# Second block: where the convolution's taps and its layer norm run, and a third buffer for loaded weights

## The chip, the cores and the metric

The kernel runs on 1 core of one Trainium2 chip. The metric is the device time of one execution in microseconds (us), a median of runs. The engines are TensorE (PE in the rows; its weight loads PEld), VectorE (DVE), ScalarE (ACT), GpSimd (POOL) and SyncE (SP), which issues nearly all DMAs in one queue, in order.

## What is computed

Three transformer-like blocks stand one behind the other, on 1024 positions of width 1024 in float32. The change touches the second block:

```python
def second_block(x, norm_g, w_in, ...):
    h = rmsnorm(x, norm_g[l])
    z = h @ w_in[l]
    qa, ka, va, glu_a, glu_b, pool_in, sgu_u, sgu_v, gates = jnp.split(z, split_at, axis=-1)
    y_a = neighborhood_attention(qa, ka, va, na_rpb[l])
    y_b = conformer_conv(glu_a, glu_b, ...)
    y_c = multiscale_pool(pool_in, pool_w[l], pool_scale[l])
    y_d = spatial_gating(jax.nn.gelu(sgu_u), jax.nn.gelu(sgu_v), ...)
    y = jnp.concatenate([y_a, y_b, y_c, y_d], axis=-1) * jax.nn.silu(gates)
    x = x + y @ w_out[l]
    return rmsnorm(x, final_g)

def conformer_conv(a, b, dw_w, dw_b, ln_g, ln_b, pw):      # 256 channels, CONV_WIDTH = 31
    h = a * jax.nn.sigmoid(b)
    h = lax.conv_general_dilated(h, dw_w[:, None, :], ..., feature_group_count=h.shape[-1]) + dw_b
    h = jax.nn.silu(layernorm(h, ln_g, ln_b))
    return h @ pw
```

## The kernel before

Activations lie feature-major: 128 features on the partitions, 1024 positions along the free axis, handled in two halves `h` of 512. Every float32 product is made of three TensorE matmuls, of a high and a low part of weights and activations (`mm3`, L190 to L192). `dense` makes one output tile of 128 x 512 from eight such triples, 24 matmuls; `dense_tm` the same for a tile with positions on the partitions, 128 x 256.

**Weights.** In the second block the weights have been split into high and low parts earlier and lie in DRAM (`wsplit`). `ready` (L159) loads one weight, 512 KB high and 512 KB low, into tiles with the tags `whi` and `wlo` of the pool `wp`, which has two buffers for each tag. A weight therefore waits until the last but one has been used. The first and third blocks use `chunk` (L147) instead: it loads an unsplit weight under the tag `raw` (two buffers of the same size), and ScalarE and VectorE or GpSimd split it into `whi` and `wlo`. Over the second block the two `raw` buffers hold the third block's first two weights.

**The second block's stages**, in program order: for each half the GLU (`glu`: two dense tiles for each of two channel groups `b`, hp = pa * sigmoid(pb)), the values of the attention (`values`, stored to `vd`), the queries and keys (`qk`, stored to `qkd`); then the pooling branch (`px`, `s2`, `s4`, `pls`), the gating's layer norm (`v2`: eight tiles of 128 x 256, `dense_tm`, Gelu into one of two `sq` buffers, then `layer_norm` on VectorE with one power on GpSimd), the loads of the attention's operands from `qkd` (`stacks(0)`, L1114, 32 DMAs of 32 x 1024), the convolution's layer norm and its 256 x 256 product (L1245 to L1272), two gate blocks (L1274 to L1289, weights 10 and 11, four dense tiles in all), and `silu(f)`, eight gates of two dense tiles each, which multiply what the branches stored in `yd`. The neighbourhood attention follows: 2 head groups x 2 bands x 4 column tiles x 4 heads, 64 score tiles of 128 x 384. A score tile is a product (L1368), bias and maximum on VectorE (L1371), an exponential on ScalarE, reciprocal and scaling on VectorE, three transposes (L1379), a copy on ScalarE, and a share of the product with the values (L1386). The bias tiles are loaded in a ring of four and get their mask on GpSimd (L1361). The table `more` puts `silu` 7, 2, 3, 0 and 1 in between the score tiles; 4, 5 and 6 stand ahead of them. Sixteen dense tiles of the output projection (`out`, with `mix`) end the block.

**The taps.** The convolution is a generator, `taps`: one tap of the centre on ScalarE (L1126), and 30 for each of two channel groups. Of these 60, 40 are one VectorE instruction each, `ca += hp * w` (L1138). The 20 with `j % 3 == 0` are a ScalarE product into a `tap` tile, which has one buffer (L1135), and a GpSimd addition into `cb` (L1136); `cb` is added to `ca` at the end (L1141). `fill(n)` takes n taps out of the generator wherever it is called.

**What sets the order.** The source order gives each instruction its place only roughly: the program is built under a scheduler that puts each engine's instructions into one fixed sequence, with priorities by program order. On the chip each engine then runs its own sequence in order, and a waiting instruction holds everything behind it on its engine. The same goes for SP's queue of DMA issues.

## Time and profile before

| | us |
|---|---|
| median of 3 runs | 3373.1 (3364.29 to 3378.03) |
| the profiled execution | 3371.98 |
| its span, first to last instruction | 3370.2 |
| TensorE busy in it | 3177.4 (94%) |
| VectorE, ScalarE, GpSimd busy | 2073.7, 1480.9, 633.5 |
| mean granted TensorE clock | 0.973 |

Times inside the profile are us from the span's start. Granted clock 1.00 is 2.4 GHz, 0.50 is 1.2 GHz, the lower level. The second block runs from about 1250 to 1800; its pooling, convolution and gate stages lie between 1345 and 1567, its attention between 1567 and 1737. A matmul's record is longer than the step to the next one, since matmuls are pipelined, so that a busy TensorE is not one at its peak.

### The profile page before, as it was taken

How to read it: one execution, taken by the hardware profiler on the slowest of the kernel's cores; microseconds unless marked ns; L12 is line 12 of the kernel's file. 1: busy time of each engine (PE TensorE's matmuls, PEld its weight loads, DVE VectorE, ACT ScalarE, POOL GpSimd, SP SyncE). 2: the span in 40 equal slices, each digit the busy share in tenths (PEclk: the TensorE clock that was granted, in tenths of full speed). 3: DMA queues.
4: the chain of work that ended last, by engine and by line, in shares of the span. 5: the costliest groups of instructions: out<-in, count | busy, mean ns of one | idle time of the engine just before them, and what ended most of it. 6: DMA issues, size and time to landing. Idle time of an engine off the chain costs nothing.

```text
span 3370.2 us, 43537 instructions
## 1 busy us (share of the span) xinstructions
PE 3177.4 (94%) x16068; PEld 2647.5 (79%) x16068; DVE 2073.7 (62%) x3779; ACT 1480.9 (44%) x2678; POOL 633.5 (19%) x427
## 2 busy tenths in 40 slices
PE   7999999999999998879999899989899999999997
PEld 6789877788888887667677778778887778888886
DVE  8666666554446554953666575675735587887436
ACT  5454553455543222322544465554534444545312
POOL 3000024000000001521213454445323200000001
PEclk9999999999999999889999899999999999999999
DMA  4112124433489726546765221224513333222433
GB/s 131 42 54 63 57 100 160 133 107 120 131 318 352 275 80 217 175 142 216 208 237 165 63 69 60 82 91 144 169 57 119 122 112 105 79 91 94 133 113 105
DMA packets 173989, 445.73 MB, mean 132 GB/s; under 512 B 22736, under 2 KB 31312, under 8 KB 169680
## 3 DMA queue, kind: packets, MB, share of 16 engines
q1 hardware_dynamic: 173776, 442.96, 40.4%
q8 instruction: 126, 2.06, 0.3%
q14 instruction: 87, 0.71, 0.1%
HBM read 329.63 MB, written 106.43 MB: 129 GB/s over the span
## 4 chain that ended last, share of the span: by engine, by line
PE 72%; DVE 12%; DMA 7%; ACT 4%; issue 3%; POOL 1%; SPq 0%; DVEq 0%; ACTq 0%; POOLq 0%
PE ps_d L190 21%; PE ps_d L192 21%; PE ps_d L191 21%; DVE ca L1138 2%; DMA wlo<-wsplit 1%; ACT whi L143 1%; DMA nq<-upd 1%; DVE wlo L145 1%; DVE act L145 1%; POOL wlo L145 1%; PE ps_o L1386 1%; DMA wsplit<-w 1%; DVE acc L1520 1%; PE ps_t L1379 1%; DMA w<-in_w_fm 1%
## 5 line engine op out<-in xcount | busy, mean ns | idle before, releaser
L190 PE MATMUL ps_d<-act,whi 128*128 128x512 f32 x1344 | 540.0, 402 | 40.1 <-DMA whi<-wsplit 24.0
L192 PE MATMUL ps_d<-act,wlo 128*128 128x512 f32 x1344 | 535.2, 400 | 7.6 <-DVE wlo L145 4.0
L191 PE MATMUL ps_d<-act,whi 128*128 128x512 f32 x1344 | 536.2, 399 | 0.1
L143 ACT ACTIVATE whi<-raw 128x1024 fp32r<-128x1024 f32 (+2 forms) x282 | 268.5, 953 | 537.9 <-PE ps_d L191 442.6
L192 PE MATMUL ps_d<-up,wlo 128*128 128x512 f32 x864 | 336.7, 390 | 2.7 <-DVE wlo L145 2.7
L145 POOL TENSOR_TENSOR wlo<-raw,whi 128x1024 fp32r<-128x1024 f32 (+1 forms) x110 | 265.9, 2420 | 384.1 <-ACT whi L143 366.9
L190 PE MATMUL ps_d<-up,whi 128*128 128x512 f32 x864 | 336.4, 390 | 0.1
L191 PE MATMUL ps_d<-up,whi 128*128 128x512 f32 x864 | 336.4, 390 | 0.0
L190 PEld LDWEIGHTS ps_d<-act,whi 128*128 128x128 f32 x1344 | 258.7, 192 | 98.7 <-issue 33.4
L191 PE MATMUL ps_d<-act,ws 128*128 128x512 f32 x812 | 316.3, 389 | 0.0
L192 PE MATMUL ps_d<-act,ws 128*128 128x512 f32 x812 | 314.4, 390 | 0.0
L190 PE MATMUL ps_d<-act,ws 128*128 128x512 f32 x812 | 312.7, 390 | 0.4 <-ACT ps_d L856 0.4
L192 PEld LDWEIGHTS ps_d<-act,wlo 128*128 128x128 f32 x1344 | 257.7, 192 | 65.1 <-DMA wlo<-wsplit 6.7
L191 PEld LDWEIGHTS ps_d<-act,whi 128*128 128x128 f32 x1344 | 258.4, 192 | 53.2 <-issue 1.1
L230 POOL TENSOR_TENSOR rr<-rv,mhalf 128x4 f32<-128x4 f32 (+1 forms) x43 | 45.6, 1059 | 1165.0 <-DVE rv L220 978.9
L145 DVE TENSOR_TENSOR wlo<-raw,whi 128x1024 fp32r<-128x1024 f32 (+2 forms) x172 | 176.5, 1026 | 108.5 <-ACT whi L143 108.1
L192 PE MATMUL ps_d<-mix,wlo 128*128 128x512 f32 x512 | 203.5, 398 | 5.6 <-POOL wlo L145 4.7
L190 PE MATMUL ps_d<-mix,whi 128*128 128x512 f32 x512 | 201.9, 400 | 5.6 <-DVE acc L646 4.3
L191 PE MATMUL ps_d<-mix,whi 128*128 128x512 f32 x512 | 204.4, 399 | 0.7 <-DVE mix L145 0.6
L192 PEld LDWEIGHTS ps_d<-up,wlo 128*128 128x128 f32 x864 | 162.3, 188 | 38.0 <-DVE wlo L145 4.2
L190 PEld LDWEIGHTS ps_d<-up,whi 128*128 128x128 f32 x864 | 162.3, 188 | 33.7 <-ACT whi L143 0.6
L191 PEld LDWEIGHTS ps_d<-up,whi 128*128 128x128 f32 x864 | 162.3, 188 | 33.4
(440 smaller groups left out, 6619.2 us busy)
## 6 DMA issues: line engine op xcount, KB each, us to landing
raw<-in_w_up SPq DMA_DIRECT2D x90, 512.0 KB, 3.9
wsplit<-w SPq DMA_DIRECT2D x32, 1024.0 KB, 5.8
raw<-in_w_fm SPq DMA_DIRECT2D x56, 512.0 KB, 3.9
upd<-c SPq DMA_DIRECT2D x108, 256.0 KB, 3.0
nq<-upd SPq DMA_DIRECT2D x108, 256.0 KB, 3.6
whi<-wsplit SPq DMA_DIRECT2D x50, 512.0 KB, 4.5
wlo<-wsplit SPq DMA_DIRECT2D x50, 512.0 KB, 5.5
xd<-acc SPq DMA_DIRECT2D x80, 256.0 KB, 3.2
```

The lines of the kernel that those rows point to most:

```text
L143: nc.scalar.activation(hi, src, AF.Copy)
L145: e.tensor_tensor(lo, src, hi.bitcast(F32), op=ALU.subtract)
L190: nc.tensor.matmul(out, lhsT=wh, rhs=xh, start=start, stop=False, skip_group_check=more)
L191: nc.tensor.matmul(out, lhsT=wh, rhs=xl, start=False, stop=False, skip_group_check=more)
L192: nc.tensor.matmul(out, lhsT=wl, rhs=xh, start=False, stop=stop, skip_group_check=more)
L230: self.nc.gpsimd.tensor_tensor(r, v, self.mhalf.broadcast_to([P, n]), op=ALU.pow)
L1138: nc.vector.scalar_tensor_tensor(ca[b][:, dst], hx[b][:, src], w, ca[b][:, dst], op0=ALU.mult, op1=ALU.add)
L1379: nc.tensor.transpose(tp[:, blk(kb)], pr[:, blk(kb)], e.ident)
L1386: nc.tensor.matmul(po[32 * hd : 32 * hd + 32, :P], lhsT=va[ct][:, band + kb, blk(hd, 32)], rhs=pts[hd][:, blk(kb)], start=kb == 0, stop=kb ...
L1520: nc.vector.scalar_tensor_tensor(m, m, g[:, k : k + 1], r, op0=ALU.mult, op1=ALU.mult)
```

## The change

Three things are edited. `ready` now turns among three places: two are the `whi`/`wlo` pairs, the third is the pair of `raw` buffers. All 60 taps are VectorE instructions, and the `fill` calls are given other counts and two more places (gate blocks, first `silu`). The convolution's layer norm and product become a generator `conv_rest`, of which two steps at a time are taken behind the halves of `silu` 5, 6 and 7; `silu(7)` moves ahead of the attention, and `silu` 2 and 3 trade places in `more`.

```diff
     def ready(self, src, shape=(8, P)):
 
-        self.turn = (self.turn + 1) % (2 + len(self.wx))
-        wp = self.wp if self.turn < 2 else self.wx[0]
+        self.turn = (self.turn + 1) % 3
         out = []
         for i, t in enumerate(("whi", "wlo")):
-            w = wp.tile([P] + list(shape), F32R, tag=t, name=t)
+            w = self.wp.tile([P] + list(shape), F32R, tag=t if self.turn < 2 else "raw", name=t)
...
         def taps():
+            w = lambda b, i: cv[:, b * 34 + i : b * 34 + i + 1]
             for b in range(2):
-                w = lambda i: cv[:, b * 34 + i : b * 34 + i + 1]
-                nc.scalar.activation(ca[b], hx[b], AF.Identity, bias=w(31), scale=w(15))
-                nc.gpsimd.memset(cb[b], 0.0)
+                nc.scalar.activation(ca[b], hx[b], AF.Identity, bias=w(b, 31), scale=w(b, 15))
             for j in range(15):
                 for b in range(2):
                     for d in (j - 15, 15 - j):
...
-                        if j % 3 == 0:
-                            t = odd.tile([P, T], F32, tag="tap", name="tap")[:, src]
-                            nc.scalar.activation(t, hx[b][:, src], AF.Copy, scale=w)
-                            nc.gpsimd.tensor_tensor(cb[b][:, dst], cb[b][:, dst], t, op=ALU.add)
-                        else:
-                            nc.vector.scalar_tensor_tensor(ca[b][:, dst], hx[b][:, src], w, ca[b][:, dst], op0=ALU.mult, op1=ALU.add)
+                        nc.vector.scalar_tensor_tensor(ca[b][:, dst], hx[b][:, src], w(b, d + 15), ca[b][:, dst], op0=ALU.mult, op1=ALU.add)
                         yield
-            for b in range(2):
-                nc.vector.tensor_tensor(ca[b], ca[b], cb[b], op=ALU.add)
...
                 qk(1, i, h)
-                fill(1)
+                fill(3)
...
                 nc.scalar.activation(x[:, half(h)], e.dense(w, hs[h]), AF.Copy)
-                fill(1)
+                fill(2)
...
-        fill(99)
         st = stacks(0)
-
-
-        cw = e.kept(io["conv_pw_2"], 2, 256)
-        for h in range(2):
...
                 nc.sync.dma_start(yd[6 + b, :, h], t)
+                fill(4)
+
+
+        def conv_rest():
+            cw = e.kept(io["conv_pw_2"], 2, 256)
+            for h in range(2):
+                bk = [e.pt() for _ in range(2)]
+                xn = e.slot("xn", (4, 256))
+                for t in range(4):
...
+                    layer_norm(e, tp[:, :256], xn[:, t], LN)
+                    for b in range(2):
+                        nc.tensor.transpose(bk[b][:, blk(t)], xn[:, t, blk(b)], e.ident)
+                    yield
...
-        for f in (4, 5, 6):
-            silu(f)
+        silu(4, lambda: fill(5))
+        fill(99)
+        steps = conv_rest()
+
+        def hook():
+            for _ in range(2):
+                next(steps, None)
+
+        for f in (5, 6, 7):
+            silu(f, hook)
+        for _ in steps:
+            pass
...
-        more = {(0, 0): (7,), (0, 1): (2, 3), (1, 0): (0, 1)}
+        more = {(0, 0): (2,), (0, 1): (3,), (1, 0): (0, 1)}
```

Three places show what becomes of this in the engines' sequences. The first is SP's queue around `stacks(0)`: `st` are the attention's operands, `lw` the gating's parameters, `yd` a branch's stored result. Before:

```order
L173 DMA nt<-in_conv_pw 128x512
L1220 DMA yd_10678<-nt 128x512
L1114 DMA st_12212<-qkd_10679 32x1024 x4
L1114 DMA st_12213<-qkd_10679 32x1024 x4
L1114 DMA st_12214<-qkd_10679 32x1024 x4
L1114 DMA st_12215<-qkd_10679 32x1024 x4
L1114 DMA st_12232<-qkd_10679 32x1024 x4
L1114 DMA st_12233<-qkd_10679 32x1024 x4
L1114 DMA st_12234<-qkd_10679 32x1024 x4
L1114 DMA st_12235<-qkd_10679 32x1024 x4
L166 DMA whi<-wsplit 128x1024
L166 DMA wlo<-wsplit 128x1024
```

SP's queue at the same place, changed:

```order
L165 DMA whi<-wsplit 128x1024
L165 DMA wlo<-wsplit 128x1024
L1209 DMA yd_10678<-nt 128x512 x3
L1215 DMA lw<-in_sgu_ln 128x512
L1216 DMA lw<-in_sgu_w 128x512
L1113 DMA st_12137<-qkd_10679 32x1024
L1209 DMA yd_10678<-nt 128x512
L1113 DMA st_12137<-qkd_10679 32x1024 x3
L1113 DMA st_12138<-qkd_10679 32x1024 x4
```

The weight of the first gate block, which stood behind the 32 loads, now stands ahead of the pooling's stores; the second gate block's weight stays behind them.

The second place is SP's queue where the third block's first two weights are loaded (`raw<-in_w_fm`). Before, that is at the start of the second block:

```order
L1229 DMA bst<-in_sgu_b 128x256
L152 DMA raw<-in_w_down 128x640 x20
L152 DMA raw<-in_w_fm 128x1024
L1054 DMA xd_10665<-acc 128x512 x2
L152 DMA raw<-in_w_fm 128x1024
L166 DMA whi<-wsplit 128x1024
L166 DMA wlo<-wsplit 128x1024
```

In the changed program they stand at the end of the second block, behind its last weight:

```order
L165 DMA whi<-wsplit 128x1024
L165 DMA wlo<-wsplit 128x1024
L1593 DMA xd_14985<-acc 128x512
L1622 DMA lvf<-in_c_levels 128x448
L1593 DMA xd_14985<-acc 128x512
L152 DMA raw<-in_w_fm 128x1024 x4
```

That last weight is the 50th which `ready` loads, and by the turn among three places it is one of those in the `raw` pair.

The third place is TensorE's sequence at the first score tiles of the attention. Before, the tiles stand between the matmuls of a `silu` tile (`ps_d<-act`):

```order
L190 MATMUL ps_d<-act,whi 128x512
L1386 MATMUL ps_o<-probT,va 32x128 x2
L1368 MATMUL ps_s<-st_12232,st_12212 128x384
L1368 MATMUL ps_s<-st_12233,st_12213 128x384
L191 MATMUL ps_d<-act,whi 128x512
L192 MATMUL ps_d<-act,wlo 128x512
L190 MATMUL ps_d<-act,whi 128x512
L1379 MATMUL ps_t<-ident,pr 128x128 x6
```

Changed, the first six tiles stand alone:

```order
L1371 MATMUL ps_s<-st_12157,st_12137 128x384
L1371 MATMUL ps_s<-st_12158,st_12138 128x384
L1371 MATMUL ps_s<-st_12159,st_12139 128x384
L1371 MATMUL ps_s<-st_12160,st_12140 128x384
L1382 MATMUL ps_t<-ident,pr 128x128 x6
L1389 MATMUL ps_o<-probT,va 32x128
L1371 MATMUL ps_s<-st_12157,st_12137 128x384
L1371 MATMUL ps_s<-st_12158,st_12138 128x384
L1389 MATMUL ps_o<-probT,va 32x128
L1382 MATMUL ps_t<-ident,pr 128x128 x6
L1389 MATMUL ps_o<-probT,va 32x128
L189 MATMUL ps_d<-act,whi 128x512
```

Six of the ten `silu` tiles that stood among the first 24 score tiles now stand ahead of the attention; the remaining four stand among score tiles 6 to 12, and tiles 12 to 44 have none, where before that was so for tiles 24 to 44.

## Rows read from the trace of the kernel before

**Rows 1.** Busy by stretch: us, PE, PEld, DVE, ACT, POOL, clock, DMA share, GB/s

```profile
1299.00:1345.00 46.00, 38.89 (x201) 32.86 (x200) 15.14 (x22) 8.42 (x17) 6.27 (x5) 0.93 0.67 217
1345.00:1424.00 79.00, 64.72 (x292) 52.84 (x290) 76.26 (x47) 25.91 (x32) 37.91 (x15) 0.87 0.57 174
1424.00:1482.00 58.00, 49.73 (x302) 44.53 (x300) 44.28 (x100) 19.75 (x29) 21.43 (x18) 0.97 0.43 130
1482.00:1500.00 18.00, 5.53 (x18) 4.17 (x19) 5.34 (x14) 0.57 (x1) 2.19 (x5) 0.54 1.02 267
1500.00:1567.00 67.00, 65.42 (x340) 53.34 (x339) 20.06 (x38) 15.91 (x24) 5.78 (x6) 1.00 0.53 171
1567.00:1640.00 73.00, 73.00 (x410) 56.26 (x409) 37.60 (x109) 30.17 (x74) 16.94 (x9) 1.00 0.69 215
1640.00:1680.00 40.00, 31.63 (x219) 20.53 (x218) 26.70 (x86) 22.67 (x63) 13.07 (x7) 0.83 0.73 212
...
1670.00:1710.00 40.00, 38.13 (x278) 25.34 (x268) 37.46 (x110) 28.65 (x78) 14.87 (x8) 0.98 0.59 187
```

**Rows 2.** TensorE's waits, 1299 to 1345 first, then 1345 to 1540: total, times, longest

```profile
PE ps_d L190 <- DMA whi<-wsplit: 4.1, 2, 3.3
...
PE ps_d L190 <- DMA whi<-wsplit: 20.6, 4, 9.1
PE ps_t L1258 <- DVE xn L1037: 5.1, 1, 5.1
PE ps_s L190 <- ACT pls L143: 4.8, 2, 4.5
```

**Rows 3.** SP's queue in order of time: start, us until issued, what

```profile
1366.14 4.14 SPq L1082 DMA_DIRECT2D vd<-nt  x6
...
1385.87 9.50 SPq L1104 DMA_DIRECT2D qkd<-qk  x2
...
1474.37 16.64 SPq L1114 DMA_DIRECT2D st<-qkd  x32
1491.84 0.34 SPq L166 DMA_DIRECT2D whi<-wsplit  x1
```

**Rows 4.** One line's instructions: count, ns min/median/max, first and last start, forms

```profile
L1138 DVE SCALAR_TENSOR_TENSOR ca<-hp,g_conv_par,ca x40: 1259/1274/3440, 1347.5 to 1424.5; 128x1010 f32<-128x1010 f32 x4, 128x1011 f32<-128x1011 f32 x4, 128x1013 f32<-128x1013 f32 x4, 128x1014 f32<-128x1014 f32 x4
L1141 DVE TENSOR_TENSOR ca<-ca,cb x2: 1218/1222/1226, 1443.7 to 1451.7; 128x1024 f32<-128x1024 f32 x2
L1210 DVE SCALAR_TENSOR_TENSOR nt<-s,g_c_iw,px x8: 743/751/2872, 1437.4 to 1466.7; 64x512 f32<-64x512 f32 x8
```

**Rows 5.** Groups, 1250 to 1900: busy us, mean ns of one, idle before

```profile
L1138 DVE SCALAR_TENSOR_TENSOR ca<-hp,g_conv_par,ca 128x1010 f32<-128x1010 f32 (+9 forms) x40 | 73.3, 1870 | 1.7 <-ACT ca L1126 1.3
...
L1135 ACT ACTIVATE tap<-hp,g_conv_par 128x1009 f32<-128x1009 f32 (+4 forms) x20 | 22.8, 1139 | 23.7 <-POOL cb L1136 23.7
```

**Rows 6.** The chain that ended last, start and us; then GpSimd's instructions

```profile
1347.55 1.28 DVE ca L1138
...
1348.86 2.88 DVE ca L1138
...
1353.07 3.27 DVE ca L1138
...
1348.69 1.97 POOL L1136 TENSOR_TENSOR cb<-cb,tap 128x1009 f32<-128x1009 f32 x1 [32.45 <-ACT tap L1135]
1351.91 3.35 POOL L1136 TENSOR_TENSOR cb<-cb,tap 128x1009 f32<-128x1009 f32 x1 [1.25 <-ACT tap L1135]
```

**Rows 7.** TensorE's instructions one by one: start and us

```profile
1340.16 0.40 PE L191 MATMUL ps_d<-act,whi 128*128 128x512 f32 x1
...
1355.37 0.39 PE L192 MATMUL ps_d<-act,wlo 128*128 128x512 f32 x1
...
1659.42 0.69 PE L1368 MATMUL ps_s<-st,st 128*128 128x384 f32 x1 [6.61 <-DVE mx L1371]
```

**Rows 8.** Score tiles on VectorE, 1567 to 1640, then 1670 to 1710

```profile
L1371 DVE CUSTOM_DVE_ANT_0 pr<-ps_s,bias x22: 551/557/559, 1567.6 to 1636.3; 128x384 f32<-128x384 f32 x22
...
L1371 DVE CUSTOM_DVE_ANT_0 pr<-ps_s,bias x23: 530/547/558, 1671.5 to 1709.3; 128x384 f32<-128x384 f32 x23
```

**Rows 9.** DMA issues of the page: KB each, us to landing; a split on ScalarE

```profile
raw<-in_w_fm SPq DMA_DIRECT2D x56, 512.0 KB, 3.9
...
1828.53 1.05 ACT L143 ACTIVATE whi<-raw 128x1024 fp32r<-128x1024 f32 x1
```

More of the change, by code (lines that the diff above doesn't have):

```diff
@@ L153, in chunk @@
         self.turn = (self.turn + 1) % (2 + len(self.wx))
-        wp = self.wp if self.turn < 2 else self.wx[0]
+        wp = self.wx[0] if self.wx and self.turn == 2 else self.wp
         hi, lo = (wp.tile(shape, F32R, tag=t, name=t) for t in ("whi", "wlo"))
@@ L159, in ready @@
     def ready(self, src, shape=(8, P)):
-        self.turn = (self.turn + 1) % (2 + len(self.wx))
-        wp = self.wp if self.turn < 2 else self.wx[0]
+        self.turn = (self.turn + 1) % 3
         out = []
         for i, t in enumerate(("whi", "wlo")):
-            w = wp.tile([P] + list(shape), F32R, tag=t, name=t)
+            w = self.wp.tile([P] + list(shape), F32R, tag=t if self.turn < 2 else "raw", name=t)
             self.nc.sync.dma_start(w.bitcast(F32), src[:, i].rearrange("p (a b) -> p a b", a=shape[0]))
@@ L1119, in block2 @@
         ca = [e.slot("ca", (T,)) for _ in range(2)]
-        cb = [e.slot("cb", (T,)) for _ in range(2)]
         hx = [t.rearrange("p a b -> p (a b)") for t in hp]
         def taps():
+            w = lambda b, i: cv[:, b * 34 + i : b * 34 + i + 1]
             for b in range(2):
-                w = lambda i: cv[:, b * 34 + i : b * 34 + i + 1]
-                nc.scalar.activation(ca[b], hx[b], AF.Identity, bias=w(31), scale=w(15))
-                nc.gpsimd.memset(cb[b], 0.0)
+                nc.scalar.activation(ca[b], hx[b], AF.Identity, bias=w(b, 31), scale=w(b, 15))
             for j in range(15):
@@ L1243, in block2 @@
             fill(1)
-        fill(99)
         st = stacks(0)
-        cw = e.kept(io["conv_pw_2"], 2, 256)
-        for h in range(2):
-            bk = [e.pt() for _ in range(2)]
-            xn = e.slot("xn", (4, 256))
-            for t in range(4):
-                tp = e.pss()
-                for b in range(2):
-                    nc.tensor.transpose(tp[:, blk(b)], ca[b][:, blk(4 * h + t)], e.ident)
-                layer_norm(e, tp[:, :256], xn[:, t], LN)
-                for b in range(2):
-                    nc.tensor.transpose(bk[b][:, blk(t)], xn[:, t, blk(b)], e.ident)
-            hl = []
-            for b in range(2):
-                o = b * 34
-                t = e.tnt()
-                nc.scalar.activation(t, bk[b], AF.Silu, bias=cv[:, o + 33 : o + 34], scale=cv[:, o + 32 : o + 33])
-                y = e.split_slot(t, "cs")
-                hl.append((y[:, 0], y[:, 1]))
-            for f in range(2):
-                p = e.pss()
-                for b in range(2):
-                    e.mm3(p, (cw[0][:, b, blk(f)], cw[1][:, b, blk(f)]), hl[b], b == 0, b == 1)
-                t = e.tnt()
-                nc.scalar.activation(t, p, AF.Copy)
-                nc.sync.dma_start(yd[2 + f, :, h], t)
         for b in range(2):
@@ L1289, in block2, with silu @@
                 nc.sync.dma_start(yd[6 + b, :, h], t)
+                fill(4)
[5 more added lines that the diff above has]
+                for t in range(4):
+                    tp = e.pss()
+                    for b in range(2):
+                        nc.tensor.transpose(tp[:, blk(b)], ca[b][:, blk(4 * h + t)], e.ident)
+                    layer_norm(e, tp[:, :256], xn[:, t], LN)
+                    for b in range(2):
+                        nc.tensor.transpose(bk[b][:, blk(t)], xn[:, t, blk(b)], e.ident)
+                    yield
+                hl = []
+                for b in range(2):
+                    o = b * 34
+                    t = e.tnt()
+                    nc.scalar.activation(t, bk[b], AF.Silu, bias=cv[:, o + 33 : o + 34], scale=cv[:, o + 32 : o + 33])
+                    y = e.split_slot(t, "cs")
+                    hl.append((y[:, 0], y[:, 1]))
+                for f in range(2):
+                    p = e.pss()
+                    for b in range(2):
+                        e.mm3(p, (cw[0][:, b, blk(f)], cw[1][:, b, blk(f)]), hl[b], b == 0, b == 1)
+                    t = e.tnt()
+                    nc.scalar.activation(t, p, AF.Copy)
+                    nc.sync.dma_start(yd[2 + f, :, h], t)
+                yield
         mix = [[None, None] for _ in range(NK)]
-        def silu(f):
+        def silu(f, hook=lambda: None):
             w = store.get("fm", 12 + f)
```

2 lines of the change are left out of this document (1 added, 1 removed).

## The prediction

> **What bounds the kernel now.** I read first the busy times by stretch [rows 1], then in each stretch that stands out TensorE's waits [rows 2], then the queue or engine named there [rows 3], and only then the lines that the diff edits [rows 4 to 6].
>
> TensorE sets the time: it is busy 3177 of 3370 us. So an edit is worth what it takes from TensorE's idle time, or from stretches in which its granted clock is low, and nothing else. In the second block both are found in a few places [rows 1]. In 1299 to 1345 TensorE is busy 38.89 of 46 us at a clock of 0.93. In 1345 to 1500 it is idle 14.3 + 8.3 + 12.5 = 35.1 us, in three stretches at 0.87, 0.97 and 0.54. Work at a clock c takes 1/c of its time at full clock, so the clock costs about 64.7 x 0.13 + 49.7 x 0.03 + 5.5 x 0.46 = 12.4 us there; 47.5 us are lost in all. In 1500 to 1567 only 1.6 us are idle, and the clock is 1.00: the place to which the change moves work has nothing to give. In 1640 to 1680 the attention idles 8.4 us at a clock of 0.83.
>
> The waits [rows 2] say what ends last: in 1299 to 1345 a loaded weight, 4.1 us; in 1345 to 1540 loaded weights again, 20.6 us in four waits, then the convolution's layer norm 5.1 and the pooled tile 4.8. So weights come first. Why are they late? SP's queue is in order [rows 3]. Stores of `vd` hold it 4.14 us and stores of `qkd` 9.50 us, since each waits for the engine that makes its tile; the 32 loads of `stacks` take 16.64 us, and the first gate block's weight is issued behind them at 1491.84: that is the 9.1 us wait. And those 32 loads stand behind the pooling and the gating's layer norm, which VectorE reaches only after the taps. VectorE is busy 76.26 of 79 us in 1345 to 1424 [rows 1]: over that stretch it is the second bound, and what it delays comes back to TensorE through SP's queue.
>
> **The change part by part.** All terms are against the profiled execution, 3372.0 us (span 3370.2), which is 1.1 us under the median of 3373.1.
>
> *Taps.* Before, 40 taps at a mean of 1.870 are 73.3 us [rows 5] and two additions of 1.22 are 2.4 [rows 4]: 75.7 us of VectorE. After, it is 60 taps and no such addition. What does one cost? The line's median is 1.274, its maximum 3.44 [rows 4]. The one-by-one rows say where the long ones come from [rows 6]: a tap beside which GpSimd does nothing takes 1.28; the tap that starts at 1348.86, 0.17 us behind a GpSimd addition of 1.97, takes 2.88; the one at 1353.07, during an addition of 3.35, takes 3.27. In the change GpSimd has no additions left in these taps, so I take the median: 60 x 1.274 = 76.4 us, or +0.7. At the old mean it would be 60 x 1.870 = 112.2, or +36.5: the upper bound, and a rival below. The pooling's L1210 shows the same pattern (median 0.751, maximum 2.872 [rows 4]) beside GpSimd; there and in its neighbours some microseconds of VectorE come back.
>
> The Trainium skill has a rule for this ("SBUF — State Buffer", section "Who interferes with whom"): a VectorE instruction with two inputs in SBUF and a GpSimd instruction that reads SBUF use one shared read path, and whichever comes second waits until the other is through. The trace agrees: the 2.88 is what is left of the 1.97, plus 1.08, and near a full tap. By this rule the sum holds 1.27 a tap, by the mean alone 1.87. The rule also speaks against any GpSimd work left in this stretch, which the sum doesn't count.
>
> Twenty ScalarE products, 22.8 us, and ScalarE's 23.7 us of waiting for GpSimd's use of the single `tap` buffer [rows 5] vanish. ScalarE writes the values that the `vd` stores wait for, so the 4.14 us hold of SP's queue should go. The 9.50 us hold comes from VectorE, which has as many taps as before in its way, and may stay.
>
> *Third buffer and the order together.* The order of the changed program puts the first gate block's weight ahead of the pooling's stores and the 32 loads; its gate block can start when the gating's layer norm is through, not at 1497. With three places a weight is asked for one dense pair earlier, some 2 x 5.45 us. A dense tile costs 24 steps of 15.21/67 = 0.227 us [rows 7] = 5.45. Two terms:
>
> - 1299 to 1345: 7.1 us idle and 38.89 x 0.07 = 2.7 of clock are at stake, of which weights are 4.1 by name. I take **-7**, bounds -10 and 0.
> - 1345 to 1500: of 47.5 us lost, the weights are 20.6 by name, the layer norm wait of 5.1 moves away with its stage, and with them goes most of the 12.4 of clock. That gives -38 if all of it went. But the pooled tile's 4.8 and the first values' wait stay, as pooling still follows the taps on VectorE, and the stores of `qkd` still hold the queue: about 8 are left. I take **-30**, bounds -15 and -38.
>
> *The convolution's layer norm between gates.* Its instructions are the same; each step is a VectorE chain with TensorE transposes on both sides. The longest wait for it before was 5.1 us [rows 2]. Now dense matmuls stand between the transposes in most steps. Nothing is gained in 1500 to 1567, which idled 1.6. I take **+2**, bounds 0 and +10 (two waits of the old kind).
>
> *The attention loses its cover.* The six dense tiles that moved ahead (6 x 5.45 = 32.7 us of TensorE) were filling the attention's chain of score, bias, exponential and transposes. With cover, 22 score tiles took 73 us, beside ten dense tiles less a few matmuls, 231 x 0.227 = 52.4: TensorE paid 20.6/22 = 0.94 us a tile [rows 7, 8]. With little cover, 23 tiles took 40 us, 1.74 each; VectorE was busy 37.46 of these 40 [rows 1, 8], so there it is the bound. Two dense tiles (10.9) stood in the 40 us; without them a tile costs 29.1/23 = 1.27. So a tile that loses its cover costs between 0.33 and 0.80 more. By the order, 6 + 12 = 18 more tiles lose it (tiles 0 to 6, and 12 to 24): 5.9 to 14.4. I take **+12**, near the upper end, since VectorE was the busy one; bounds 0 and +25 (the upper is explained at the second rival).
>
> *The seam to the third block.* The second block's last weight lies in the `raw` pair, and the third block's first two weights, which were loaded a whole block ahead, now come behind it. The chain that is then open: issue and landing 3.9, the split on ScalarE 1.05 [rows 9], the low part about as much again, and some 2 at the lower clock once TensorE restarts: **+7**, bounds +4 and +10.
>
> Sum: -7 - 30 + 2 + 12 + 7 = -16. **3372 - 16 = 3356 us.**
>
> **The rivals.** *First: nothing is given back.* If the attention's chain is refilled by the output tiles and the seam's loads go out early, the +12 and +7 fall to about +3, and the 1345 to 1500 stretch gives its whole -38: -7 - 38 + 2 + 3 = -40, **3332 us**. For it: VectorE and ScalarE lose interference all over the stretch. Against it: the queue order at the seam, which is fixed.
>
> *Second: the attention starves once more.* Where the head group changes, the score tile waited 6.61 us for a bias [rows 7], which its DMA brought behind the loads for that group in SP's queue, and the stretch's clock was 0.83 [rows 1], 31.63 x 0.17 = 5.4 of clock. If the uncovered attention gets one more such stop, that is 12 more, and the attention costs +24: -7 - 30 + 2 + 24 + 7 = -4, **3368 us**. For it: 32 tiles in a row without cover consume bias tiles faster than before.
>
> *Third: the change doesn't do what it says.* The third buffer lets a weight be asked for earlier only if SP's queue gets to the request; if the stores of `qkd` and the values still hold it, 1299 to 1345 gives -2 and the next stretch -15: -17 + 2 + 12 + 7 = +4, **3376 us**. Nor are the taps spread: in the changed order all 60 stand ahead of the gating's layer norm on VectorE, so that the new places at the gate blocks find none left. For it: the holds of 4.14 and 9.50 [rows 3]. Against: the biggest of the four waits is the gate block's, and in the changed order its weight has moved.
>
> *Fourth, slower: taps stay at 1.87.* If GpSimd is not what stretches them but the full VectorE or the shifted operands, VectorE gets 36.5 more right ahead of the pooling and the layer norm, and all behind it is late by that: -16 + 36 = +20, **3392 us**. It decides from about 1.27 + 16/60 = 1.54 us a tap, where the gain is gone. Against it: the fast taps of 1.26 to 1.28 are the majority, and have the same operands.
>
> **How the numbers follow.** About 0.5% (16.9 us) is what a measurement of this kernel can tell from no change; that puts the bounds at 3356 and 3390. My forecast has a chance of 0.48 (with its own spread, 3340 to 3368), the first rival 0.19, the second 0.16, the third 0.11, the fourth 0.06. Faster: half of the forecast's cases, the first rival and a little of the second, 0.24 + 0.19 + 0.05 = 0.48. Slower: the fourth, and the third's upper tail, 0.06 + 0.04 = 0.10. Same: the rest, 0.42. The range leaves out the fourth rival and the outer half of the first: 3330 to 3382.
>
> **What would show each step right or wrong.** (1) The tap line: 60 instructions with a mean near 1.27; near 1.87, the fourth rival is right. (2) The first gate block's dense tile: about 1460 where it was 1497, 30 us earlier after what is saved ahead of it; no wait for a weight over 2 us in 1345 to 1480. (3) The waits for weights in 1299 to 1345 gone; if not, the third rival. (4) The attention: tiles 12 to 44 at about 1.7 us with VectorE over 90% busy; another wait of some 6 us for a bias and a clock near 0.8 would show the second rival. (5) The seam: one idle stretch of 5 to 6 us on TensorE behind the last output tile, waiting for `raw` and its split. (6) TensorE's busy time stays near 3177 less what the clock gives back; a change in it of more than 20 us would mean a clock effect that I have not counted. The prediction is wrong in sign if VectorE, not TensorE, turns out to end last in 1345 to 1500 with more than its old 76 us of taps.

## The result and the profile after

The changed kernel takes 3348.0 us (median of 4 runs, 3346.1 to 3350.8), where the kernel before took 3371.5 beside it: a ratio of 0.993, with a 95% interval of 0.992 to 0.994, or 23.5 us less. The forecast was 3356, with a range of 3330 to 3382 and "faster" as the likeliest sign. The mechanism was right; in the profiled execution two terms had the wrong size and their errors partly cancelled, and the credit inside the largest term was given to the wrong edit, as the experiments show.

The profiled execution has a span of 3349.0 us. The busy times of the same stretches as in [rows 1] (us, TensorE, its weight loads, VectorE, ScalarE, GpSimd, granted clock, DMA share, GB/s):

```profile
1299.00:1345.00 46.00, 46.00 (x254) 40.04 (x253) 26.94 (x31) 10.41 (x18) 5.17 (x4) 1.00 0.79 263
1345.00:1424.00 79.00, 76.13 (x412) 65.61 (x410) 75.49 (x86) 14.14 (x24) 1.35 (x4) 1.00 0.62 198
1424.00:1482.00 58.00, 50.26 (x303) 43.30 (x304) 32.18 (x80) 8.97 (x18) 5.36 (x9) 0.91 0.61 174
1482.00:1500.00 18.00, 18.00 (x82) 14.86 (x81) 6.20 (x12) 2.43 (x4) 0.54 (x1) 1.00 0.59 203
1500.00:1567.00 67.00, 60.38 (x274) 47.88 (x273) 23.44 (x58) 17.86 (x32) 8.63 (x9) 0.94 0.57 190
1567.00:1640.00 73.00, 65.90 (x408) 45.35 (x408) 51.06 (x145) 38.00 (x101) 25.37 (x14) 0.87 0.78 226
1640.00:1680.00 40.00, 38.56 (x244) 26.77 (x243) 33.51 (x91) 23.96 (x65) 13.91 (x8) 0.93 0.51 167
```

Up to 1500 most of what TensorE had lost to idle time and clock is gone: in 1345 to 1424 it now runs 412 matmuls at a clock of 1.00, where it ran 292 at 0.87. What is left in 1345 to 1500 is 10.6 us of idle time and, by the prediction's way of counting, 4.5 of clock, 15.1 of the 47.5. From 1555 on, where the attention now begins, it is the other way round: in 1567 to 1640 TensorE is busy 65.90 us at 0.87, where it was 73.00 of 73 at 1.00. The same is in TensorE's waits, in 1345 to 1540 first (against [rows 2]), then in 1540 to 1760 (us in total, times, longest):

```profile
PE ps_s L189 <- ACT pls L143: 6.2, 3, 3.6
PE ps_d L189 <- DMA whi<-wsplit: 2.9, 1, 2.9
...
PE ps_t L1382 <- DVE sm L1378: 8.2, 5, 5.4
PE ps_t L1382 <- DVE pr L1379: 4.1, 4, 1.4
PE ps_s L1371 <- DVE mx L1374: 2.3, 3, 1.4
```

Weights cost 2.9 us in one wait instead of 20.6 in four, the layer norm's 5.1 is gone, and the pooled tile's wait stayed (6.2, before 4.8). In exchange the attention waits for its own chain, on reciprocal and scaling (L1378, L1379), above all 5.4 us at its first tiles.

SP's queue in 1345 to 1510 answers to [rows 3] (start, us until issued, what):

```profile
1348.42 6.89 SPq L1081 DMA_DIRECT2D vd<-nt  x6
...
1357.11 1.09 SPq L1081 DMA_DIRECT2D vd<-nt  x2
...
1385.01 3.27 SPq L1103 DMA_DIRECT2D qkd<-qk  x2
...
1410.84 0.32 SPq L165 DMA_DIRECT2D whi<-wsplit  x1
...
1420.00 16.06 SPq L1209 DMA_DIRECT2D yd<-nt  x3
...
1444.84 16.96 SPq L1113 DMA_DIRECT2D st<-qkd  x31
1462.64 0.34 SPq L165 DMA_DIRECT2D whi<-wsplit  x1
```

The longest hold by a store of `qkd` is 3.27 us, where one was 9.50. The first gate block's weight is the one issued at 1410.84, ahead of the `st` loads; the one behind them, at 1462.64, is the second gate block's, for which TensorE waits the 2.9 us. What holds the queue longest ahead of the `st` loads is now the pooling's stores of `yd` (L1209), 16.06 us; two of the same stores held it 8.62 us before.

The taps, against [rows 4], count and ns min/median/max:

```profile
L1129 DVE SCALAR_TENSOR_TENSOR ca<-hp,g_conv_par,ca x60: 1252/1273/1284, 1336.9 to 1425.5; 128x1009 f32<-128x1009 f32 x4, 128x1010 f32<-128x1010 f32 x4, 128x1011 f32<-128x1011 f32 x4, 128x1012 f32<-128x1012 f32 x4
```

Sixty at a median of 1.273 us, and not one of them over 1.284. They end at 1426.8, about where the forty ended before (the last started at 1424.5).

At the seam to the third block, the end of TensorE's last output tile and what follows. First the changed kernel, then the kernel before:

```profile
1771.52 0.39 PE L191 MATMUL ps_d<-mix,wlo 128*128 128x512 f32 x1
1774.23 1.94 PE L215 MATMUL ps_t<-ident,sums 128*128 128x128 f32 x8 [2.32 <-DVE sums L307]
1776.49 0.80 PE L189 MATMUL ps_d<-act,whi 128*128 128x512 f32 x1 [0.33 <-ACT whi L143]
```

```profile
1800.01 0.39 PE L192 MATMUL ps_d<-mix,wlo 128*128 128x512 f32 x1
1801.27 0.47 PE L190 MATMUL ps_d<-act,whi 128*128 128x512 f32 x1 [0.87 <-ACT whi L143]
```

The first dense tile of the third block follows 0.87 us behind the last output tile before, and 4.6 us after.

### The profile page after: what moved, and what is told of

The parts are those of the page before. It is cut to its first block, busy times and chain, and to the rows that moved or that the text cites. A ratio compares the mean times of both kernels' runs of the same rounds, so it can differ in the third digit from the quotient of the medians.

```text
span 3349.0 us, 43514 instructions
## 1 busy us (share of the span) xinstructions
PE 3176.1 (95%) x16068; PEld 2648.6 (79%) x16068; DVE 2074.7 (62%) x3797; ACT 1456.1 (43%) x2655; POOL 579.1 (17%) x405
## 4 chain that ended last, share of the span: by engine, by line
PE 40%; DVE 6%; ACT 3%; issue 2%; POOL 1%; DMA 1%; SPq 0%; DVEq 0%; ACTq 0%; POOLq 0%
PE ps_d L189 12%; PE ps_d L191 12%; PE ps_d L190 12%; ACT whi L143 1%; DVE acc L1523 1%; PE ps_s L1806 1%; POOL wlo L145 0%; DVE hSA L1807 0%; DVE hE L1792 0%; PE ps_t L1382 0%; PE ps_o L1389 0%; DVE act L145 0%; DVE acc L1524 0%; PE ps_d L1817 0%; DVE pr L1719 0%
## 5 line engine op out<-in xcount | busy, mean ns | idle before, releaser
L189 PEld LDWEIGHTS ps_d<-act,whi 128*128 128x128 f32 x1344 | 257.1, 191 | 75.2 <-issue 10.9
L229 POOL TENSOR_TENSOR rr<-rv,mhalf 128x4 f32<-128x4 f32 (+1 forms) x43 | 46.2, 1075 | 1186.1 <-DVE rv L219 999.0
```

The costliest lines, as they stand in the source:

```text
L189: nc.tensor.matmul(out, lhsT=wh, rhs=xh, start=start, stop=False, skip_group_check=more)
L229: self.nc.gpsimd.tensor_tensor(r, v, self.mhalf.broadcast_to([P, n]), op=ALU.pow)
```

## The experiments

The first four kernels undo or do parts of the change alone. Theory A held that the gain comes with the weights (buffer and order), rival B that it is VectorE's and ScalarE's, rival C that it is the order's. Prices below are differences of medians; the kernel before has 3371 to 3372 in each comparison, the changed one 3348.0, measured in the first comparison only. Runs of one kernel spread over some 5 to 12 us, so a difference of less than some 4 us between medians tells nothing.

**The third buffer alone.** Only `ready` is edited:

```
-        self.turn = (self.turn + 1) % (2 + len(self.wx))
-        wp = self.wp if self.turn < 2 else self.wx[0]
+        self.turn = (self.turn + 1) % 3
...
-            w = wp.tile([P] + list(shape), F32R, tag=t, name=t)
+            w = self.wp.tile([P] + list(shape), F32R, tag=t if self.turn < 2 else "raw", name=t)
```

> The kernel before (3371.5 us) with the third buffer alone. Theory A, the gain ahead of the attention is that of loaded weights (20.6 us of TensorE's waits in 1345 to 1540 and 4.1 ahead of it): the waits in 1299 to 1345 go (-8 to -10) and the two of about 5 us behind the stores of qkd shrink (-6 to -10 with their clock); the gate block's 9.1 us wait stays, as its weight is still issued behind the 32 loads; the seam costs +7. Sum -8 to -13, about 3361. Rival B, the gain is VectorE's and ScalarE's, freed of GpSimd's additions: the buffer gives 1299 to 1345 at most and the seam takes it back, 3369 to 3376.

Measured: 3362.6 us, ratio 0.997 (0.996 to 0.998): -9.6. Two readings go against the expectation or beyond it. In 1345 to 1540 TensorE's waits are these:

```profile
PE ps_d L189 <- DVE qk L1101: 9.0, 2, 7.9
PE ps_s L189 <- ACT pls L143: 8.8, 3, 4.5
PE ps_t L1257 <- DVE xn L1036: 4.1, 2, 2.1
PE ps_d L189 <- DMA whi<-wsplit: 3.8, 2, 3.2
```

The first gate block's weight is no longer waited for at all. It is issued at 1427.97, ahead of the 32 loads at 1458.38, and the block's first dense tile starts at 1463.4 instead of 1497.1: the buffer alone brings it forward, with the order as before. The 3.2 us are for the second gate block's weight, which is issued behind those loads, at 1476.04. Theory A had the first weight still behind them. And the time that the loads gave back is met by a new wait, 7.9 us for the queries and keys that VectorE makes behind its taps (L1101). The weights had hidden that VectorE was late too.

**All taps on VectorE, alone.** The taps of the changed kernel in the program order of before, with its `fill` counts:

```
-                        if j % 3 == 0:
-                            t = odd.tile([P, T], F32, tag="tap", name="tap")[:, src]
-                            nc.scalar.activation(t, hx[b][:, src], AF.Copy, scale=w)
-                            nc.gpsimd.tensor_tensor(cb[b][:, dst], cb[b][:, dst], t, op=ALU.add)
-                        else:
-                            nc.vector.scalar_tensor_tensor(ca[b][:, dst], hx[b][:, src], w, ca[b][:, dst], op0=ALU.mult, op1=ALU.add)
+                        nc.vector.scalar_tensor_tensor(ca[b][:, dst], hx[b][:, src], w(b, d + 15), ca[b][:, dst], op0=ALU.mult, op1=ALU.add)
```

> The kernel before with all 60 taps on VectorE alone, the fill counts and the place of the layer norm as before. Both theories: 60 taps at 1.27 us, 76 us. Theory A: VectorE ends as late as before, ScalarE's 24 us of waiting vanish, so the store of the values holds SP's queue less; -3 to -8, about 3366, and the waits for weights keep at least 15 of their 20.6 us. Rival B: most of the change's 23 us come from here, 3350 to 3356.

Measured: 3360.5 us, ratio 0.997 (0.995 to 0.998): -11.6, between the two. SP's queue shows what changed:

```profile
1361.61 4.14 SPq L1082 DMA_DIRECT2D vd<-nt  x6
...
1410.47 2.68 SPq L1104 DMA_DIRECT2D qkd<-qk  x2
...
1464.20 16.43 SPq L1114 DMA_DIRECT2D st<-qkd  x32
1481.00 0.34 SPq L166 DMA_DIRECT2D whi<-wsplit  x1
```

Against theory A, the 4.14 us hold by the values' stores, which I had put down to ScalarE's waiting, is still there (and the changed kernel has one of 6.89). They are six stores, and two that need not wait take 1.09 us, so by an estimate from these rows some 3.3 of the 4.14 are the issuing itself. It is the stores of `qkd` that no longer hold the queue: 2.68 us at most, before 9.50. VectorE's instructions around that store, in the kernel before and with the taps alone, say why (start, us, count):

```profile
1373.09 19.14 DVE L1138 SCALAR_TENSOR_TENSOR ca<-hp,g_conv_par,ca 128x1017 f32<-128x1017 f32 x9
1392.16 2.87 DVE L1096 TENSOR_TENSOR qk<-nt,qk 128x512 fp32r<-128x512 f32 x1
```

```profile
1381.18 0.69 DVE L1096 TENSOR_TENSOR qk<-nt,qk 128x512 fp32r<-128x512 f32 x1 [6.09 <-ACT qk L1095]
1381.79 4.83 DVE L1130 SCALAR_TENSOR_TENSOR ca<-hp,g_conv_par,ca 128x1012 f32<-128x1012 f32 x4
```

Before, nine taps took 19.14 us, 2.13 each, and the `qk` behind them took 2.87; it ended at 1395.0, where the store's hold of [rows 3] ends. With the taps alone VectorE was through with the taps ahead of it and waited 6.09 us for `qk`, which then took 0.69, and the store is issued in 1.05. These rows argue that the gain comes from VectorE being early and not from the work that ScalarE lost; no run takes away ScalarE's products alone. The first gate block's weight is again issued behind the 32 loads, and 14.8 us of waits for weights are left.

**The order alone.** The changed kernel with the taps and `ready` of the kernel before; the edits left are, in the main, these (the `fill` counts and places and the body of `conv_rest` are not shown):

```
-        for f in (4, 5, 6):
-            silu(f)
+        silu(4, lambda: fill(5))
+        fill(99)
+        steps = conv_rest()
...
+        for f in (5, 6, 7):
+            silu(f, hook)
...
-        more = {(0, 0): (7,), (0, 1): (2, 3), (1, 0): (0, 1)}
+        more = {(0, 0): (2,), (0, 1): (3,), (1, 0): (0, 1)}
```

> The changed kernel with the taps as before (20 on ScalarE and GpSimd) and two places for weights: only the order is changed (layer norm of the convolution between the gates, silu 7 ahead of the attention, fill counts). Theory A: the 9.1 us wait and the 5.1 us wait of the layer norm go, with some 8 of clock (-20), the attention gives back 12 to 18: 3364 to 3370. Rival C, the order is the whole gain: 3345 to 3352.

Measured: 3377.8 us, ratio 1.0015 (1.0005 to 1.0025): +5.6, slower. Both theories missed. TensorE's longest wait, 10.5 us, is still for the first gate block's weight:

```profile
PE ps_d L190 <- DMA whi<-wsplit: 22.5, 4, 10.5
```

So the order does not bring that weight forward. Of the 50 weights that `ready` loads, 24 are issued ahead of the 32 loads in every kernel here with two buffers, in the old order and in the new, and 25 in every kernel with three, again in either order. The first gate block's weight is the 25th. That the 5.6 us lost are what the order takes from the attention's cover is an inference; the run on the cover below bears on it.

**The changed kernel without the third buffer.** `ready` as before, all else changed.

> The changed kernel (3348.0 us) without the third buffer. Theory A: the 10 us of 1299 to 1345 and some of the waits behind it come back, +12 to +18, less the seam's 7: 3353 to 3359. Rival B: within 4 us of the changed kernel or faster than it by the seam's 7, 3341 to 3350.

Measured: 3366.7 us, ratio to before 0.9985 (0.9976 to 0.9995), 18.7 slower than the changed kernel: beyond theory A's 3353 to 3359, and against rival B. The longest wait for a weight is 11.4 us, again for the first gate block's, and 1299 to 1345 is back at 39.55 us busy and a clock of 0.89.

**GpSimd beside the taps.** Two kernels add work on GpSimd at the 20 places among the 60 taps of the changed kernel where the kernel before had additions: once additions, which read two tiles, once memsets, which only write. In the source both stand beside the taps; where GpSimd runs them the traces have to say.

```
+                        if j % 3 == 0:
+                            nc.gpsimd.tensor_tensor(cb[b][:, dst], cb[b][:, dst], hx[b][:, src], op=ALU.add)
                         yield
```

> The changed kernel with 20 additions on GpSimd (ca-sized, two inputs in SBUF, into tiles that nothing reads) beside the taps, at the places where the kernel before had them; the result does not use them. Theory, a tap is stretched by a GpSimd instruction that runs beside it: the taps' mean rises from 1.27 to 1.7 to 1.9 us, VectorE is 25 to 35 us later, and the kernel loses 10 to 25: 3358 to 3373. Rival, the old mean of 1.87 came from the other work of the kernel before: taps stay at 1.27 and the time within 3 us of 3348.

Measured: 3378.6 us, 30.6 more than the changed kernel: more than the theory's range.

```
+                        if j % 3 == 0:
+                            nc.gpsimd.memset(cb[b], 0.0)
                         yield
```

> The changed kernel with 20 memsets of 128x1024 on GpSimd beside the taps, at the places where the run before it had additions: GpSimd is busy there and writes SBUF, but reads nothing. Theory, what stretches a tap is GpSimd's reading: the 60 taps stay between 1.25 and 1.29 us, and the time stays near 3348. Rival, any GpSimd instruction on SBUF holds VectorE: taps rise towards 2 us as with the additions (3378.6).

Measured: 3344.4 us in one run, near the changed kernel's. The taps beside the additions (count, ns min/median/max):

```profile
L1131 DVE SCALAR_TENSOR_TENSOR ca<-hp,g_conv_par,ca x60: 1251/1267/3395, 1337.6 to 1460.1; 128x1009 f32<-128x1009 f32 x4, 128x1010 f32<-128x1010 f32 x4, 128x1011 f32<-128x1011 f32 x4, 128x1012 f32<-128x1012 f32 x4
```

The start of that stretch, VectorE and GpSimd (start, us, count):

```profile
1337.64 15.09 DVE L1131 SCALAR_TENSOR_TENSOR ca<-hp,g_conv_par,ca 128x1009 f32<-128x1009 f32 x5 [1.31 <-ACT ca L1125]
...
1336.47 15.19 POOL L1133 TENSOR_TENSOR cb<-cb,hp 128x1009 f32<-128x1009 f32 x5 [19.41 <-DVE hp L1071]
```

The taps of the kernel with memsets, and those memsets (ns min/median/max, first and last start):

```profile
L1131 DVE SCALAR_TENSOR_TENSOR ca<-hp,g_conv_par,ca x60: 1253/1272/1286, 1334.8 to 1424.5; 128x1009 f32<-128x1009 f32 x4, 128x1010 f32<-128x1010 f32 x4, 128x1011 f32<-128x1011 f32 x4, 128x1012 f32<-128x1012 f32 x4
```

```profile
L1133 POOL MEMSET cb<- x20: 952/954/960, 1314.4 to 1334.6; 128x1024 f32 x20
```

Beside additions five taps and five additions take the same 15 us, some 3 us for each pair, as if the two engines took turns. The 20 additions are over at 1400.8; the taps that had none beside them kept 1.27 (the median), and the last tap starts 35 us later than in the changed kernel. So additions on GpSimd stretch the taps, and without them the taps are short.

The memsets did not do what they were meant to. They wait for nothing, and GpSimd ran them all from 1314.4 to 1335.5, ahead of the taps; only the last one overlaps a tap, the first, by 0.67 us, and that tap took 1.27. Beside the others ran one `qk` instruction of VectorE with two inputs (L1095), which took 0.69 us, as without memsets. So that GpSimd's reading stretches a tap, and not its being busy or its writing, is not shown for the taps as a whole, and the time of this run says nothing about it. The Trainium skill ("SBUF — State Buffer", section "Who interferes with whom") says that a VectorE instruction with two inputs in SBUF contends with a GpSimd instruction that reads SBUF, and not with one that only writes it; the prediction's "any GpSimd work" went further than that. The run with additions agrees with the first half, 3 us a pair where a tap alone takes 1.27; for the second half there are only the 1.27 and the 0.69 just named.

Of the price of 30.6 us the largest part is one wait: TensorE stands 20.0 us for one weight, whose request stands behind a store of `qkd` that holds SP's queue 29.62 us:

```profile
1372.05 29.62 SPq L1103 DMA_DIRECT2D qkd<-qk  x2
1401.76 0.39 SPq L165 DMA_DIRECT2D whi<-wsplit  x1
```

**The attention's cover.** The changed kernel with `silu` 7 back among the score tiles:

```
-        silu(4, lambda: fill(5))
         fill(99)
         steps = conv_rest()
...
-        for f in (5, 6, 7):
+        for f in (4, 5, 6):
             silu(f, hook)
...
-        more = {(0, 0): (2,), (0, 1): (3,), (1, 0): (0, 1)}
+        more = {(0, 0): (7,), (0, 1): (2, 3), (1, 0): (0, 1)}
```

> The changed kernel (3348.0 us) with silu 7 back in the attention and 2, 3 behind it, as before the change; the convolution's layer norm goes between the halves of silu 4, 5 and 6 instead of 5, 6 and 7. Theory: the six dense tiles taken from the attention cost it 12 to 18 us; two of them come back here, and silu 3 moves ahead by a band, so -4 to -10, 3338 to 3344, with less of the low clock that stands in 1570 to 1655. Rival: the attention is bound by VectorE whatever stands beside it, and the give-back has another cause: within 3 us of 3348.

Measured: 3338.7 us, ratio to before 0.990 (0.9885 to 0.992), 9.3 less than the changed kernel, as the theory said. In 1555 to 1640 the changed kernel (first row) and this one (second):

```profile
1555.00:1640.00 85.00, 71.87 (x428) 48.60 (x427) 57.94 (x162) 42.21 (x113) 27.18 (x15) 0.84 0.78 234
```

```profile
1555.00:1640.00 85.00, 77.67 (x507) 55.34 (x506) 57.69 (x173) 45.28 (x122) 28.64 (x16) 0.95 0.77 230
```

VectorE is as busy in both; TensorE runs 507 instead of 428 matmuls, 5.8 us busier and at a clock of 0.95 instead of 0.84. The two windows lie at different places of the attention, though, since it starts at 1543.3 here and at 1553.7 in the changed kernel. So take the whole of it, from the first score tile to the end of the last output tile:

```profile
1543.27:1763.23 219.96, 202.10 (x1185) 149.63 (x1183) 150.42 (x380) 96.85 (x240) 50.05 (x30) 0.95 0.70 226
```

In the changed kernel that is 218.2 us (its row stands in the next section), here 220.0 with two dense tiles, 10.9 us, more to do: 9.1 less, which is the 9.3 of the medians.

**Third buffer and taps, in the order of before.** Both edits, without the new order.

> The kernel before with the third buffer and all taps on VectorE, the layer norm and the silu tiles where they were. Alone the two gave -9.6 and -11.6, the order alone +5.6. Theory, the order costs its cover and the other two carry the gain, more than their sum because the wait behind the stores of qkd was handed from the buffer to VectorE: 3340 to 3348, as fast as the changed kernel or faster. Rival, the order is needed for the rest of the change's gain: 3351 to 3356 (the sum of the two is 3351).

Measured: 3347.7 us, ratio 0.993 (0.991 to 0.995): the same as the changed kernel. With both of the other edits, the order as it was made is worth nothing (0.3 us). The sum of the two alone was 3351, which is within the spread of its runs (3343.4 to 3352.2), so that they are worth more together is not shown; but the wait of 9.0 us for `qk` that the buffer alone had uncovered is gone. The first gate block's dense tile starts at 1448.4, in the order of before. TensorE still waits 4.6 us for the second gate block's weight here, and 2.1 and 2.0 us in the layer norm.

**The seam.** One line at the second block's start shifts the turn, so that the 48th weight lies in the `raw` pair, and the last does not:

```
     save_x(0)
+    e.turn = 2
     e.psum_split()
```

> The changed kernel with the turn among the three places shifted at the second block's start, so that its 48th weight and not its last lies in the raw pair. Theory, the seam costs 4 to 7 us since the third block's first weights wait for the last output tile: their loads start some 11 us earlier, 3341 to 3344, and the first dense tile of the third block follows without a wait for its split weight. Rival, the wait there is the final norm's on VectorE (2.3 us): within 2 us of 3348.

Measured: 3339.8 us, ratio to before 0.990 (0.9885 to 0.992), 8.2 less than the changed kernel, a little more than expected. The first dense tile of the third block:

```profile
1766.11 0.47 PE L189 MATMUL ps_d<-act,whi 128*128 128x512 f32 x1 [0.87 <-ACT whi L143]
```

Its busy times in 1740 to 1800:

```profile
1740.00:1800.00 60.00, 57.53 (x270) 47.33 (x269) 38.66 (x60) 26.34 (x36) 20.79 (x13) 1.00 0.53 182
```

It follows after 0.87 us as it did before the change, and the clock is 1.00 over 1740 to 1800, where the changed kernel had 54.94 us busy at 0.91. The wait of 2.32 us for the norm's sums that stood at this place in the changed kernel is gone too: with the weight there, a dense tile runs in its place. So it was no cost of its own.

**Both gains together, and two variants.** First the changed kernel with the cover and the seam's shift:

> The changed kernel with both of the edits that gained apart: silu 7 back among the score tiles (-9.3) and the 48th weight, not the last, in the raw pair (-8.2). If the two costs are separate, as the theory has it, they add: 3348 - 17 = 3331. If the seam's start is set by the attention's end and the norm instead, they don't: 3336 to 3340.

Measured: 3331.8 us (3327.6 to 3334.6), ratio to before 0.9885 (0.987 to 0.990). The two add (9.3 + 8.2 = 17.5, measured 16.2): the cover is worth 8.0 with the shift in place, and the shift 6.9 with the cover. It is the fastest of all kernels here, 39 us under the one before. Next, third buffer, taps and shift in the order of before:

> The kernel before with the third buffer, all taps on VectorE and the shifted turn; the layer norm and the silu tiles where they were. The seam's 6 to 8 us come off 3347.7: 3340 to 3342. Against the run with both edits on the changed order it shows what the new place of the layer norm is worth once the attention has its cover: the theory, which puts the waits for the layer norm at 2 + 2 us and its clock, expects this one 5 to 10 us slower than that.

Measured: 3339.1 us, 7.3 slower than the one above. Once the attention keeps its cover, the convolution's new place gains what the old one loses: waits of 4.5 us for the second gate block's weight and 2.1 and 2.0 us in the layer norm, and a clock of 0.89 in 1424 to 1500. Last, `silu` 6 goes back among the score tiles too, and the convolution's steps move ahead to the second gate block and `silu` 4 and 5:

```
                 nc.sync.dma_start(yd[6 + b, :, h], t)
+                if b:
+                    hook()
...
-        for f in (4, 5, 6):
+        for f in (4, 5):
             silu(f, hook)
...
-        more = {(0, 0): (7,), (0, 1): (2, 3), (1, 0): (0, 1)}
+        more = {(0, 0): (6, 7), (0, 1): (2, 3), (1, 0): (0, 1)}
```

> As the run with both edits, and silu 6 goes back among the score tiles too: the convolution's steps stand behind the second gate block and silu 4 and 5. Theory, each pair of dense tiles given back to the attention saves some 4 to 6 us until VectorE is covered: 3322 to 3328. Rival, the price is that of the first score tiles, which stand alone in all these orders (5.4 us idle and a stretch at the lower clock), not of the number of tiles behind them: within 3 us of the run with both edits.

Measured: 3337.6 us, where the theory had 3322 to 3328 and the rival at most 3 us to either side of 3331.8. Its runs (3329.3 to 3340.3) overlap those with `silu` 6 ahead (3327.6 to 3334.6), so it gains nothing, and whether it loses is not clear. The waits at the first score tiles did shrink (3.9 to 1.1 and 1.0 us), but the waits for weights grew, here from 1424 to 1800 in the run with both edits and in this one:

```profile
PE ps_d L189 <- DMA whi<-wsplit: 4.3, 2, 2.2
```

```profile
PE ps_d L189 <- DMA whi<-wsplit: 6.2, 2, 3.6
...
PE ps_d L191 <- DMA wlo<-wsplit: 2.8, 1, 2.8
```

With 0.5 us for `wlo` in the first kernel too, weights cost 4.8 us there and 9.0 here, 4.2 more; but the waits for the pooled tile fell from 7.2 to 4.2. Why those weights come later, and whether this holds beyond the profiled execution, no run here tells.

## Why the prediction came out as it did

*What bounds the kernel* stands: TensorE's idle time and its clock in 1299 to 1500 were the place to gain, and of the 47.5 us that the prediction counted in 1345 to 1500 about 15 are left.

*Taps, +0.7 us of VectorE:* the size of a tap was right, 60 at 1.273, and so was the reason: it was GpSimd's additions that stretched them, shown by the run that puts additions back (that reading does it, and not any work on GpSimd, rests on one tap beside a memset, as said above). The +0.7 itself mixes two countings: 76.4 is a sum of durations, and the 73.3 for the 40 taps is busy time, in which records that overlap count once. By busy time the 60 taps take 73.6 against the 75.7 of before, so VectorE's sum did not rise. The conclusion drawn from it was wrong. Because VectorE's sum stays about equal, the prediction let the hold of 9.50 us "stay" and gave the taps hardly a share. But alone they gave 11.6 us. What counted was not the sum but how late VectorE's other work came out: nine taps of 2.13 us and a `qk` of 2.87 held SP's queue 9.50 us, and with taps of 1.27 the same store is issued in about 1. The 4.14 us hold of the values' stores, which the prediction expected to go with ScalarE's waits, did not go (6.89 in the changed kernel): by the estimate above most of the 4.14 is six stores being issued. It cost TensorE no wait for a weight in the changed kernel, whose only such wait in 1345 to 1540 is the 2.9 us at 1468.0.

*1299 to 1345, -7:* measured from the rows, the 7.1 us idle and the 2.7 of clock both went, -9.8. It was the bound that I had given as -10. Without the third buffer both come back.

*1345 to 1500, -30:* too small. The attention's first score tile starts at 1553.7 instead of 1567.2, and 32.7 us of dense tiles more lie ahead of it: 46.2 us gained up to there. Less the 9.8 that leaves 36.4, against -28 forecast for this term and the next together. The first gate block's first dense tile started at 1449.9 (1497.1 before; about 1460 expected). The prediction gave this to "third buffer and order together". It was buffer and taps. With the buffer alone the tile starts at 1463.4, with buffer and taps in the old order at 1448.4; with the taps alone at 1486.3, and with the order alone at 1493.5, behind a wait of 10.5 us. The prediction's sign of "no wait for a weight over 2 us" missed by the 2.9 us for the second gate block's weight, which stands in SP's queue behind the `st` loads, and these behind the pooling's stores that hold it 16.06 us.

*The convolution's layer norm between gates, +2:* in 1500 to 1555 TensorE idles 0.6 us, so it was hidden, and this term was about nothing.

*The attention's cover, +12:* too small in the profiled executions. From the first score tile to the end of the last output tile it was 233.2 us before, and is 218.2 with 32.7 us less to do: +17.7. The rows of those two stretches say of what, the changed kernel first:

```profile
1553.70:1771.90 218.20, 200.16 (x1137) 146.17 (x1135) 153.77 (x376) 95.62 (x238) 50.17 (x30) 0.91 0.67 218
```

```profile
1567.20:1800.40 233.20, 222.34 (x1281) 165.76 (x1279) 150.07 (x383) 100.98 (x245) 50.44 (x30) 0.97 0.71 226
```

Idle: 18.0 against 10.9 us, so +7.2. Clock: 200.16 x 0.09 = 18.0 against 222.34 x 0.03 = 6.7, so +11.3. My price of 0.33 to 0.80 us a tile came from a stretch that ran at a clock of 0.98 (1670 to 1710 in [rows 1]), so it held the idle time and not the clock. The second rival's particular stop, a wait for a bias at the change of the head group, fell away instead (1.4 us the longest for `mx`). That the cover was the cause is shown by the run that gave two of the tiles back: -9.3.

But 17.7 is the price in one execution, the slowest of the changed kernel's four. Five other kernels here have the same four `silu` tiles among their score tiles, and in them this stretch takes 209.9 to 216.0 us, so +9.4 to +15.5 against the 233.2. The one that differs from the changed kernel only in the turn's shift:

```profile
1553.20:1765.20 212.00, 195.40 (x1137) 141.92 (x1135) 146.87 (x377) 97.09 (x240) 49.92 (x30) 0.94 0.72 232
```

The forecast of +12 lies among these, so whether the term was too small is open. Of the signs named for it, one came true and one nearly: tiles 12 to 44 took 1.71 us each, with VectorE busy 47.24 of their 54.90 us, 86% where over 90% was named.

*The seam, +7:* right. The gap grew by 3.7 us (0.87 to 4.6), and the profile has 6.8 us at the lower clock from 1774 on, which cost 3.4: 7.1, and the shift of the turn took back 8.2.

Together 46.2 - 17.7 - 7.1 = 21.4, of the spans' difference of 21.2 in this pair of executions. The errors in them, 11 us too little gained ahead and 6 too little given back behind, cancelled in part.

*The rivals:* the first (nothing is given back, 3332) was wrong as a forecast, but is close to what the kernel gives once the seam's cost and part of the cover's are taken out, 3331.8. Of the third, one half was right: the taps are not spread to the gate blocks, the last starts at 1425.5, ahead of them. The fourth was settled by the maximum of 1.284 us.

## What to carry to other kernels

Before moving work between engines, look at how long the same instruction takes while the other engine is busy: equal sums of busy time can hide that stores behind it leave late, and that an in-order queue hands this to the next load. Work that is pulled forward out of a stage is also that stage's cover, and its price there includes the lower clock of the idle stretches, which must be read from a stretch that has them. And when a buffer is borrowed from a neighbouring stage, choose which turn uses it last: one line at the seam was worth 8 us more, beside a change that gained 23.

## What was not expected of the hardware

Taps and GpSimd additions that run at once took 15.09 us for five and 15.19 for five, some 3 us a pair, though the same tap alone takes 1.27, as if the two engines took turns; the one tap that ran beside a GpSimd memset, for 0.67 us, kept 1.27. And in the attention of the changed kernel, where waits of mostly 1 to 5 us are spread over the stretch, the clock averaged 0.91 between 1553 and 1772, with six stretches at the lower level: 18.0 us lost by the clock beside 18.0 us of idle time, where the kernel before lost 6.7 beside 10.9. In the other kernels with the same tiles in the attention it averaged 0.91 to 0.95.
